# Stick-breaking attention: keys in pairs of 512-blocks, with PSUM banks regrouped to hold the pairs

## The chip, the cores and the metric

One core of one Trainium2 chip runs one program, a whole decoder block. The metric is the device time of one execution in microseconds (us). A kernel is timed several times and the median counts; one more execution is profiled, and its trace shows every instruction of the engines: TensorE (PE in the rows; its weight loads are PEld), VectorE (DVE), ScalarE (ACT), GpSimd (POOL) and SyncE (SP), which issues most of the DMAs.

## What is computed

The block has one input projection, an attention of 8 heads and a pooling branch beside each other, one output projection, and a SwiGLU FFN. The sequence has 2048 tokens, the model 1024 channels, a head 64. The change is in the attention, which for a query t and keys s < t is

```
z = q . k / sqrt(64)
w[t,s] = sigmoid(z[t,s]) * product over s < j < t of sigmoid(-z[t,j])
out[t] = sum over s of w[t,s] * v[s]
```

The reference writes it with logarithms (log_sigmoid and a reversed cumsum); the kernel forms the running product itself, from the last key to the first.

## The kernel before

**Stages.** The program projects the tokens (q, k, v and the pooling input u), then runs the attention with the rest of the projection woven into it, then the output projection, and then the FFN, whose products are arranged as seven instead of eight. The order of the instructions on TensorE, VectorE, ScalarE and GpSimd is the order in which the Python code issues them (tc.manual_schedule); only the waits are set by the framework. Each engine works through its own list in that order, so what stands behind a waiting instruction waits too.

**Units and steps of the attention.** A unit is (h, tb, sc): head h, a block of 512 queries tb, a block of 512 keys sc, with sc from tb down to 0, since the product runs backwards. A unit has four steps i, one for each 128 queries. There are 80 units and so 320 steps. In a diagonal unit (sc == tb) a step has only (i + 1) * 128 keys; in the others it has 512. The loop at L953 issues for step n, in this order:

- weights_step (L792), for step n: two matmuls write the scores z into one PSUM bank (L801, L802; q is held as a high and a low part), and a third adds the causal mask in diagonal units (L804). ScalarE writes sigmoid(z/8) into the SBUF tile sg (L806) and then sigmoid(-z/8) over z in its PSUM bank (L807).
- scan_step (L810), for the step before (it waits until two are in the list, L960): VectorE forms the running product pr with one tensor_tensor_scan over z, from the last key to the first, starting with the first column of the same rows' product in the key block to the right (prevs) or with 1 (L818). GpSimd sets the column right of the product (L815 or L817) and multiplies sg by the shifted product: w (L821).
- values_step (L839), up to LAG turned tiles late: two matmuls add w times v into the bank av (L848, L849), for the high and the low part of w. After the last of a (head, query block), ScalarE copies av out (L853) and SP stores it.
- turn_step (L825), OFF = 7 steps late: TensorE turns up to four 128x128 squares of w into one PSUM bank wt (L833); ScalarE copies the high part wth out (L59), VectorE subtracts it from wt to get the low part wtl (L60).
- filler: pieces of the projection that is left, each of three matmuls (L69 to L71) into the bank mm. How many go into a step follows from the costs at L959 and L967 (2.5 for a step of a diagonal unit, 4.0 for another), so that they end with unit END = 78 of 80. Their results are evacuated by ScalarE, VectorE and GpSimd within the same steps.

**Banks.** All of the program uses one PSUM pool with eight banks of 512 fp32 columns: three for z (ZB), two for wt (WB), one mm, two av. In SBUF the attention has five buffers of sg, six of pr and eleven of w.

**Ends.** The first products of the output projection (mix_pieces) are woven into the last steps of the attention, three pieces a step (PER_STEP).

Of the kernel before, what the change touches and what calls it, by code (L numbers as in the profile page):

```python
# [17 lines left out]
P = 128  # L18
# [26 lines left out]
def block_kernel(ctx, tc, x, c, w_cond, b_cond, g_mix_pre, g_mix_post, w_in, w_pool,  # L45
# [93 lines left out]
    psp = ctx.enter_context(tc.tile_pool(name="ps1", bufs=2, space=PSUM, reuse_waits="tile"))  # L139
# [629 lines left out]

    att = open_pool(ph1, "att", bufs=2)  # L770
# [17 lines left out]
    qts, prevs, avs, wss = {}, {}, {}, {}  # L788
# [3 lines left out]
    def weights_step(u, i):  # L792

        h, tb, sc = u
        diag = sc == tb
        kt, qt = kv[h, sc][0], qts[h, tb]
        L = (i + 1) * P if diag else TB
        nm = f"{h}_{tb}_{sc}_{i}"
        z = z_ps(f"z{nm}")
        keys = kt[:, 0:L]  # L800
        nc.tensor.matmul(z[:, 0:L], qt[:, 0, i * P:(i + 1) * P], keys, start=True, stop=False)  # L801
        nc.tensor.matmul(z[:, 0:L], qt[:, 1, i * P:(i + 1) * P], keys, start=False, stop=not diag)  # L802
        if diag:
            nc.tensor.matmul(z[:, i * P:L], ident_r, neg_r, start=False, stop=True)  # L804
        sg = att.tile([P, TB], F32, tag="sg", bufs=5, name=f"sg{nm}")
        nc.scalar.activation(sg[:, 0:L], z[:, 0:L], AF.Sigmoid, scale=0.125)  # L806
        nc.scalar.activation(z[:, 0:L], z[:, 0:L], AF.Sigmoid, scale=-0.125)  # L807
        scans.append((u, i, z, sg, L, nm))

    def scan_step(u, i, z, sg, L, nm):  # L810

        diag = u[1] == u[2]
        pr = att.tile([P, TB + 1], F32, tag="pr", bufs=6, name=f"pr{nm}")
        if diag:
            nc.gpsimd.memset(pr[:, L:L + 1], 1.0)  # L815
        else:
            nc.gpsimd.tensor_copy(pr[:, L:L + 1], prevs[i][:, 0:1])  # L817
        nc.vector.tensor_tensor_scan(pr[:, 0:L][:, ::-1], z[:, 0:L][:, ::-1], sg[:, 0:L],  # L818
                                     one if diag else prevs[i][:, 0:1], ALU.mult, ALU.bypass)
        w = att.tile([P, TB], F32, tag="w", bufs=OFF + 4, name=f"w{nm}")  # L820
        nc.gpsimd.tensor_tensor(w[:, 0:L], sg[:, 0:L], pr[:, 1:L + 1], ALU.mult)  # L821
        prevs[i] = pr
        wss.setdefault(u, []).append(w)
# [748 lines left out]
```

## Time and profile before

| | |
|---|---|
| median of 3 runs | 2350.9 us (2348.78 to 2353.78) |
| the profiled execution | 2351.43 us, of which the trace spans 2349.6 us |
| granted TensorE clock, mean | 0.991 |
| TensorE busy over the span | 97% |
| VectorE, GpSimd, ScalarE busy | 70%, 55%, 50% |
| attention, first score matmul to last one | 323.5 to 854.3 us |

Busy time is the union of the instructions' spans on an engine. A matmul's span goes from its start to the modelled end of its pipeline, and the next one starts before that, so the busy share of TensorE says little about how much room it has; the distances between starts say more. On the other engines, too, an instruction starts a little before the one ahead of it has ended. A row of a group gives the mean span of one instruction; the advance, from one start to the next, is read from the timeline.

### The profile page before, as it was taken

Reading aid. Unit: us, or ns where it says so; the run is one execution under the profiler, and the core shown is the slowest. Engines: PE = TensorE matmul, PEld = TensorE weight load, DVE = VectorE, ACT = ScalarE, POOL = GpSimd, SP = SyncE. Lnnn points to the kernel's source line nnn. Section 1 sums busy time; section 2 is a strip of 40 time slices with the busy share of each in tenths; the row PEclk is TensorE's granted clock in tenths of the full one; section 3 lists DMA queues with packets and bytes.
Section 4 is the critical chain, followed back from the end, with each engine's and each line's share of the span. In section 5 each row is a group of like instructions: output and inputs, shape, how many; then the busy total and the mean of one; then the engine's idle time right before and its main releaser. Section 6 shows DMA issues by size and latency. Waiting matters only on the chain.

```text
span 2349.6 us, 33532 instructions
## 1 busy us (share of the span) xinstructions
PE 2278.4 (97%) x10717; PEld 1866.6 (79%) x10717; DVE 1638.0 (70%) x2221; ACT 1179.3 (50%) x2411; POOL 1293.3 (55%) x1429
## 2 busy tenths in 40 slices
PE   6999999999999989999999999999999999999997
PEld 3778878888888768887888888788888888888885
DVE  6764549999999975757565565886776565555556
ACT  4323659899998864444222232454533323234444
POOL 4542337787677764544777778430475665641004
PEclk9999999999999999999999999999999999999998
DMA  8785764333443636656554555776763333327554
GB/s 287 244 293 193 273 189 117 90 105 90 126 113 95 190 99 196 220 193 203 163 167 153 162 161 179 264 243 201 257 196 101 119 110 95 114 86 279 193 196 144
DMA packets 307116, 405.18 MB, mean 172 GB/s; under 512 B 19254, under 2 KB 179578, under 8 KB 303868
## 3 DMA queue, kind: packets, MB, share of 16 engines
q1 hardware_dynamic: 302620, 400.68, 52.8%
q10 hardware_dynamic: 4320, 2.36, 0.4%
q8 instruction: 85, 1.39, 0.2%
q14 instruction: 91, 0.75, 0.1%
HBM read 274.51 MB, written 128.45 MB: 171 GB/s over the span
## 4 chain that ended last, share of the span: by engine, by line
PE 79%; DVE 7%; issue 4%; ACT 4%; POOL 3%; DMA 3%; SPq 0%; DVEq 0%; POOLq 0%; ACTq 0%
PE t_u L70 3%; PE t_u L69 3%; PE t_u L71 3%; PE t_g L70 3%; PE t_g L69 3%; PE t_g L71 3%; PE wt L833 3%; PE dn0p L70 3%; PE dn0p L71 3%; PE dn0p L69 3%; PE dn1p L70 3%; PE dn1p L69 3%; PE dn1p L71 3%; DVE pr L818 3%; PE b_g L70 2%
## 5 line engine op out<-in xcount | busy, mean ns | idle before, releaser
L821 POOL TENSOR_TENSOR w<-sg,pr 128x512 f32<-128x512 f32 (+2 forms) x320 | 306.1, 956 | 143.6 <-DVE pr L818 81.3
L1179 POOL TENSOR_TENSOR s<-s,cu 128x512 f32<-128x512 f32 x88 | 132.7, 1515 | 240.7 <-DVE cu L1178 140.1
L818 DVE TENSOR_TENSOR_SCAN pr<-z,pr,sg 128x512 f32<-128x512 f32 x192 | 244.5, 1274 | 0.5 <-POOL pr L817 0.5
L60 DVE TENSOR_TENSOR wtl<-wt,wth 128x512 fp32r<-128x512 f32 (+1 forms) x320 | 190.3, 595 | 35.0 <-ACT wth L59 33.0
L806 ACT ACTIVATE sg<-z 128x512 f32<-128x512 f32 (+2 forms) x320 | 175.0, 547 | 48.0 <-PE z L804 22.2
L59 ACT CAST wth<-wt 128x512 fp32r<-128x512 f32 (+1 forms) x320 | 173.1, 541 | 21.5 <-PE wt L833 19.8
L833 PE MATMUL wt<-ident,w 128*128 128x128 f32 x1088 | 172.0, 273 | 2.5 <-DVE wtl L60 2.2
L807 ACT ACTIVATE z<-z 128x512 f32<-128x512 f32 (+2 forms) x320 | 174.1, 544 | 0.0
L60 DVE TENSOR_TENSOR u_s_l<-u_s,u_s_h 128x512 fp32r<-128x512 f32 x66 | 66.4, 1007 | 151.9 <-ACT u_s_h L59 151.9
L833 PEld LDWEIGHTS wt<-ident,w 128*128 128x128 f32 x1088 | 133.5, 140 | 32.6 <-DVE wtl L60 3.7
L1169 ACT ACTIVATE s<-s 128x512 f32<-128x512 f32 x88 | 55.7, 633 | 192.6 <-DVE s L1168 192.6
L801 PE MATMUL z<-kt,qt 128*128 128x512 f32 (+2 forms) x320 | 128.8, 403 | 16.8 <-DVE pr L818 12.2
L70 PE MATMUL dn0p<-w0p_l,g0p_h 128*128 128x512 f32 x308 | 121.2, 394 | 1.9 <-DVE w0p_l L60 1.9
L848 PE MATMUL av<-wth,vt 128*128 128x512 f32 (+1 forms) x320 | 121.5, 380 | 0.0
L60 DVE TENSOR_TENSOR u_a_l<-u,u_a_h 128x512 fp32r<-128x512 f32 x66 | 77.4, 1175 | 62.3 <-ACT u_a_h L59 62.3
L69 PE MATMUL dn0p<-w0p_h,g0p_h 128*128 128x512 f32 x308 | 120.5, 391 | 0.0
L71 PE MATMUL dn0p<-w0p_h,g0p_l 128*128 128x512 f32 x308 | 120.4, 391 | 0.0
L59 ACT CAST g_s_h<-g_s 128x512 fp32r<-128x512 f32 x66 | 39.5, 620 | 157.6 <-POOL g_s L1111 81.5
L849 PE MATMUL av<-wtl,vt 128*128 128x512 f32 (+1 forms) x320 | 116.9, 365 | 0.0
L802 PE MATMUL z<-kt,qt 128*128 128x512 f32 (+2 forms) x320 | 116.7, 365 | 0.0
L59 ACT CAST u_s_h<-u_s 128x512 fp32r<-128x512 f32 x66 | 38.6, 614 | 152.2 <-POOL u_s L1111 152.2
L70 PE MATMUL dn1p<-w1p_l,g1p_h 128*128 128x512 f32 x292 | 114.4, 392 | 0.0
(655 smaller groups left out, 7266.2 us busy)
## 6 DMA issues: line engine op xcount, KB each, us to landing
g<-in_w_gate_dram SPq DMA_DIRECT2D x42, 512.0 KB, 4.6
u<-in_w_up_dram SPq DMA_DIRECT2D x42, 512.0 KB, 5.0
wc<-in_w_cond_dram SPq DMA_DIRECT2D x32, 512.0 KB, 5.8
qt<-qd SPq DMA_DIRECT2D x64, 256.0 KB, 3.9
wd<-in_w_down_dram SPq DMA_DIRECT2D x44, 256.0 KB, 3.0
tdt<-wd SPq DMA_DIRECT2D x44, 256.0 KB, 2.0
w0p<-tdt SPq DMA_DIRECT2D x44, 256.0 KB, 2.9
w1p<-tdt SPq DMA_DIRECT2D x44, 256.0 KB, 2.8
```

The lines of the kernel that those rows point to most:

```text
L59: nc.scalar.copy(hi, src)
L60: low.tensor_tensor(lo, src, raw(hi), ALU.subtract)
L69: nc.tensor.matmul(ps, lh, rh, start=first and i == 0, stop=False)
L70: nc.tensor.matmul(ps, lh, rl, start=False, stop=False)
L71: nc.tensor.matmul(ps, ll, rh, start=False, stop=last and i == n - 1)
L801: nc.tensor.matmul(z[:, 0:L], qt[:, 0, i * P:(i + 1) * P], keys, start=True, stop=False)
L806: nc.scalar.activation(sg[:, 0:L], z[:, 0:L], AF.Sigmoid, scale=0.125)
L807: nc.scalar.activation(z[:, 0:L], z[:, 0:L], AF.Sigmoid, scale=-0.125)
L818: nc.vector.tensor_tensor_scan(pr[:, 0:L][:, ::-1], z[:, 0:L][:, ::-1], sg[:, 0:L], one if diag else prevs[i][:, 0:1], ALU.mult, ALU.bypass)
L821: nc.gpsimd.tensor_tensor(w[:, 0:L], sg[:, 0:L], pr[:, 1:L + 1], ALU.mult)
L833: nc.tensor.transpose(wt[:, i * P:(i + 1) * P], wss[u][i][:, b * P:(b + 1) * P], ident)
L1179: nc.gpsimd.tensor_tensor(s, s, u, ALU.mult)
```

## The change

A unit now has a list of key blocks: per head ((0, (0,)), (1, (0, 1)), (2, (1, 2)), (2, (0,)), (3, (2, 3)), (3, (0, 1)))), so two neighbouring blocks of 512 keys go together wherever there are two. That makes 48 units and 192 steps. A pair's step writes its scores into two neighbouring PSUM banks (the tile zz), has one sigmoid each way over up to 1024 columns and one scan over them; GpSimd still makes one w for each block. The product that goes on to the next unit is copied into a small tile (carry).

The loop's order changes too. The scan is issued in the step of its scores, not one step later. A step of a pair turns two tiles (each step still turns the share of a unit OFF = 5 steps back), and the two subtractions wtl are issued behind the scan of the step. Values are taken as long as more than LAG tiles wait.

PSUM is split into three pools, one after the other. In the attention there are two buffers of zz (four banks), two wt, one mm and one av, where there were three z, two wt, one mm and two av. SBUF buffers: sg three (each twice as wide), pr three (twice as wide), w six for a unit's first block and eight for its second. The costs by which the filler is spread, its end, and the places where the first output products are loaded, split and multiplied are set anew. The projection ahead of the attention, the output projection's other tiles and the FFN compute the same with the same number of instructions; their banks are taken in turn from eight tags of one bank each.

```diff
-OFF = 7
+OFF = 5
 ZB, WB = 3, 2
+WBUFS = 6, 8
...
+    psst.close()
+    psst = ExitStack()
+    psp = psum_pool(psst, "ps2")
+    z_ps = lambda name: psum("av", 1, name)
+    av_ps = z_ps
+
+    def zz_ps(name):
+        return psp.tile([P, 2, TB], F32, tag="zz", bufs=2, name=name)
...
     def weights_step(u, i):
...
+        zz = zz_ps(f"z{nm}")
+        for p, sc in enumerate(blocks):
+            diag = sc == tb
+            L = (i + 1) * P if diag else TB
+            z, keys = zz[:, p], kv[h, sc][0][:, 0:L]
+            nc.tensor.matmul(z[:, 0:L], qt[:, 0, i * P:(i + 1) * P], keys, start=True, stop=False)
+            nc.tensor.matmul(z[:, 0:L], qt[:, 1, i * P:(i + 1) * P], keys, start=False, stop=not diag)
+            if diag:
+                nc.tensor.matmul(z[:, i * P:L], ident_r, neg_r, start=False, stop=True)
+        W = (len(blocks) - 1) * TB + L
+        z = zz.rearrange("p b k -> p (b k)")[:, 0:W]
+        sg = att.tile([P, 2 * TB], F32, tag="sg", bufs=3, name=f"sg{nm}")
+        nc.scalar.activation(sg[:, 0:W], z, AF.Sigmoid, scale=0.125)
+        nc.scalar.activation(z, z, AF.Sigmoid, scale=-0.125)
...
     def scan_step(u, i, z, sg, W, nm):
...
+        pr = att.tile([P, 2 * TB + 1], F32, tag="pr", bufs=3, name=f"pr{nm}")
+        carry = carries.pop(i, None)
+        if carry is None:
+            nc.gpsimd.memset(pr[:, W:W + 1], 1.0)
         else:
+            nc.gpsimd.tensor_copy(pr[:, W:W + 1], carry)
+        nc.vector.tensor_tensor_scan(pr[:, 0:W][:, ::-1], z[:, ::-1], sg[:, 0:W],
+                                     one if carry is None else carry, ALU.mult, ALU.bypass)
+        if blocks[0]:
+            carries[i] = att.tile([P, 1], F32, tag=f"carry{i}", bufs=2, name=f"carry{nm}")
+            nc.gpsimd.tensor_copy(carries[i], pr[:, 0:1])
+        for p in range(len(blocks)):
+            cols = slice(p * TB, min((p + 1) * TB, W))
+            w = att.tile([P, TB], F32, tag=f"w{p}", bufs=WBUFS[p], name=f"w{nm}_{p}")
+            nc.gpsimd.tensor_tensor(w[:, 0:cols.stop - cols.start], sg[:, cols],
+                                    pr[:, cols.start + 1:cols.stop + 1], ALU.mult)
...
+    units = [(h, tb, blocks) for h in range(HEADS) for tb, blocks in
+             ((0, (0,)), (1, (0, 1)), (2, (1, 2)), (2, (0,)), (3, (2, 3)), (3, (0, 1)))]
+    cost = {1: 1.7, 2: 3.5}
+    area = [cost[len(blocks)] - (0.6 if blocks[-1] == tb else 0) for _, tb, blocks in units]
...
-    END = 78
+    END = 0.965
...
-    PER_STEP = 3
+    PER_STEP = 2
...
             weights_step(u, i)
-            spent += 2.5 if u[1] == u[2] else 4.0
-        if len(scans) > 1 or n >= len(steps) and scans:
-            scan_step(*scans.pop(0))
-        if len(waiting) > LAG:
+            spent += area[n // 4]
+        while len(waiting) > LAG:
             values_step(*waiting.pop(0))
         if n >= OFF:
-            u, b = steps[n - OFF]
-            waiting.append((u, b, *turn_step(u, b)))
-        goal = START + (N_PIECES - START) * spent / (4 * sum(area[:END]))
+            u, i = steps[n - OFF]
+            for m in range(i * len(u[2]), (i + 1) * len(u[2])):
+                parts, low = turn_step(u, m // 4, m % 4)
+                waiting.append((u, m // 4, m % 4, *parts))
+                turned_lows.append(low)
+        if scans:
+            scan_step(*scans.pop(0))
+        while turned_lows:
+            turned_lows.pop(0)()
+        goal = START + (N_PIECES - START) * spent / (4 * END * sum(area))
```

More of the change, by code (lines that the diff above doesn't have):

```diff
@@ L786, in block_loads @@
         return qt
-    qts, prevs, avs, wss = {}, {}, {}, {}
+    qts, carries, avs, wss = {}, {}, {}, {}
     scans = []
     def weights_step(u, i):
[L794 to L808, printed above, removed]
@@ L857, in unit_loads @@
     def unit_loads(u):
-        h, tb, sc = u
-        if sc == tb:
+        h, tb, blocks = u
+        if blocks[-1] == tb:
             qts[h, tb] = block_loads(h, tb)
@@ L949, in mix_pieces @@
                 count -= 1
-    waiting = []
+    waiting, turned_lows = [], []
     spent = 0.0
```

70 lines of the change are left out of this document (38 added, 32 removed).

## The prediction

> **What bounds the kernel now.** I read the page first, then the table of stretches, then the waits and the groups by shape of the attention, and last the timeline of a few microseconds in it.
>
> ```profile
> PE   6999999999999989999999999999999999999997
> ...
> DVE  6764549999999975757565565886776565555556
> ```
>
> The 40 slices are 58.7 us each. TensorE is at nine tenths nearly everywhere; VectorE is there with it only in slices 7 to 14, the attention. The profiled execution took 2351.43 us, 0.5 above the median of the runs (2350.9), so I add to the former and leave the 0.5 alone. The stage in stretches:
>
> ```profile
> 370.00:822.00 452.00, 442.92 (x2535) 368.84 (x2534) 428.17 (x548) 406.66 (x898) 331.82 (x606) 1.00 0.41 118
> 822.00:840.00 18.00, 15.35 (x86) 11.78 (x85) 17.08 (x23) 15.58 (x35) 16.41 (x27) 1.00 0.66 205
> 840.00:860.00 20.00, 15.77 (x82) 11.57 (x81) 20.00 (x24) 17.01 (x35) 14.38 (x24) 1.00 0.32 96
> 323.30:860.00 536.70, 517.32 (x2943) 427.92 (x2942) 506.53 (x647) 479.52 (x1056) 392.79 (x716) 1.00 0.41 119
> ```
>
> The columns are length, then busy time of PE, PEld, DVE, ACT, POOL, then granted clock, DMA share, GB/s. The last row is the attention: 536.7 us for eight heads, **67.1 us a head**, with PE busy 517.3, DVE 506.5, ACT 479.5. Two engines are full at once, so taking work from VectorE alone gives little; TensorE leaves at most 536.7 - 517.3 = 19.4 us.
>
> ```profile
> DVE wtl L60 <- ACT wth L59: 27.3, 60, 2.3
> ...
> PEld wt L833 <- DVE wtl L60: 3.7, 4, 2.7
> ```
>
> These are two waits of the attention (total us, times, longest). VectorE's largest is for ScalarE's high part, 27.3 us in all. TensorE's turns wait for a bank of the turned weights to be read (wtl) four times in 320 steps; this row matters below.
>
> **The change part by part.**
>
> ```profile
> L821 POOL TENSOR_TENSOR w<-sg,pr 128x512 f32<-128x512 f32 x224 | 244.8, 1093 | 102.3 <-DVE pr L818 59.3 <-ACT sg L806 20.9 <-ACT wth L59 3.4
> L818 DVE TENSOR_TENSOR_SCAN pr<-z,pr,sg 128x512 f32<-128x512 f32 x192 | 244.5, 1274 | 0.5 <-POOL pr L817 0.5
> ...
> L60 DVE TENSOR_TENSOR wtl<-wt,wth 128x512 fp32r<-128x512 f32 x220 | 148.6, 675 | 23.4 <-ACT wth L59 22.0
> L806 ACT ACTIVATE sg<-z 128x512 f32<-128x512 f32 x224 | 137.0, 611 | 30.4 <-PE z L802 18.6 <-PE z L804 6.6 <-POOL pr L815 1.4
> ...
> L818 DVE TENSOR_TENSOR_SCAN pr<-z,ones,sg 128x128 f32<-128x128 f32 x32 | 15.1, 473 | 0.0
> ...
> L806 ACT ACTIVATE sg<-z 128x128 f32<-128x128 f32 x32 | 9.6, 299 | 4.0 <-PE z L804 3.1 <-POOL pr L817 0.6
> ```
>
> ```profile
> 404.90 1.27 DVE L818 TENSOR_TENSOR_SCAN pr<-z,pr,sg 128x512 f32<-128x512 f32 x1
> ...
> 406.09 0.66 DVE L60 TENSOR_TENSOR wtl<-wt,wth 128x512 fp32r<-128x512 f32 x1
> ...
> 406.67 1.27 DVE L818 TENSOR_TENSOR_SCAN pr<-z,pr,sg 128x512 f32<-128x512 f32 x1
> ```
>
> *Fewer scans.* A scan costs (1274 - 473) / 384 = 2.09 ns a column. In the timeline one of 512 columns advances VectorE by 406.09 - 404.90 = 1.19 us, of which 512 x 2.09 = 1.07 are columns and 0.12 is fixed. 320 scans become 192 with the same columns: 128 x 0.12 = **15 us less on VectorE**. A scan over 1024 columns and two banks is in no row. Its bounds are the 1.27 of one bank and twice that, 2.55; I take the line, 1.27 + 1.07 = 2.34, which lies nearest to the two.
>
> *Fewer sigmoids.* (611 - 299) / 384 = 0.81 ns a column, so 1024 columns take 0.61 + 0.42 = 1.03 us (bounds 0.61 and 1.22). Against 2 x 0.61 that takes at most 0.19 off each of 256 merges, less where they overlap. ScalarE isn't last, so I credit nothing.
>
> *GpSimd* makes the same 320 products; 128 settings of a single column go and 64 carries of a single column come, beside its idle time: nothing.
>
> *TensorE* issues exactly as many instructions as before. *One value bank:* ScalarE's copy of av now has to end before the next block's first value matmul; that comes a whole step later, behind turns, filler and scores, while the copy has only the step's two sigmoids ahead of it, so I cost it at nothing (its cover is that step of over 2 us; without it up to 1 us, 31 times). DMAs and their places by step are the same; head and tail I take as they are, up to 5 us either way (PE's idle time in the two tail stretches is 2.65 + 4.23 us).
>
> *The new order* is what decides. In each step VectorE now does the scan, then the subtractions of the tiles turned in that step, and a pair's step turns two tiles through the two wt banks. So TensorE can turn the next step's second tile only when VectorE has ended this step's second subtraction, which stands behind this step's scan. Behind those turns on TensorE stand the filler and then the scores of the step after next, whose sigmoids and scan follow. That closes a **loop of two steps**. Its prices:
>
> ```profile
> 754.19 0.39 PE L849 MATMUL av<-wtl,vt 128*128 128x512 f32 x1
> 754.20 0.59 PEld L833 LDWEIGHTS wt<-ident,w 128*128 128x128 f32 x4
> ...
> 754.42 0.60 PE L833 MATMUL wt<-ident,w 128*128 128x128 f32 x4
> ...
> 754.78 0.48 PE L69 MATMUL u<-hth,wu_h 128*128 128x512 f32 x1
> ...
> 755.56 0.40 PE L801 MATMUL z<-kt,qt 128*128 128x512 f32 x1
> ...
> 757.75 0.39 PE L802 MATMUL z<-kt,qt 128*128 128x512 f32 x1
> ...
> 758.24 0.60 ACT L806 ACTIVATE sg<-z 128x512 f32<-128x512 f32 x1 [0.45 <-PE z L802]
> ...
> 758.73 0.59 ACT L807 ACTIVATE z<-z 128x512 f32<-128x512 f32 x1
> ```
>
> A matmul advances TensorE by 0.23 (754.19 to 754.42), four turns by 0.36, a filler piece of three matmuls by 0.78 (754.78 to 755.56). A weight load comes 0.22 ahead of its turn. The wait from the end of a score matmul (757.75 + 0.39) to the sigmoid is 0.10, and I take 0.2 for the loop's three changes of engine together. Filler: the code has 24 products of 8 pieces, 192, and START puts 31 of them ahead of the attention; 161 are left in it, 161 x 0.78 = 126 us, spread by the new costs, which add up to 60 a head: 126 / 480 = 0.26 us for a unit of cost.
>
> Per head 24 steps, in three classes of eight:
>
> - *Pair of key blocks, two tiles turned* (880 columns on average). Scan 0.12 + 880 x 0.00209 = 1.96. Subtractions: full tiles 0.58 + 0.67, with the narrow tiles of the diagonal 1.10. Hops 0.2 and weight load 0.22. Four turns or fewer, 0.30. Filler 3.1 x 0.26 = 0.82. Four score matmuls and the mask, 0.97 to the end of the last. Sigmoids: the first advances by 0.49 for 512 columns, 0.79 for 880, and the second takes 0.91: 1.70. Together 7.27, **3.64 a step**. TensorE's own work is 3.2 (scores 0.87, values 0.84, turns 0.68, filler 0.82), VectorE's 3.0.
> - *One key block, two tiles turned* (416 columns). The same sum: 0.99 + 1.15 + 0.42 + 0.33 + 0.37 + 0.57 + 0.93 = 4.76, 2.38 a step; TensorE's own work is 2.37. Two limits as near as that add up a little: 2.5.
> - *Pair of key blocks, one tile turned.* The second wt bank takes the wait out of the loop. TensorE has 2.4, VectorE 2.5; over the 95% that VectorE reached in the middle (428.17 of 452.00), 2.6.
>
> 8 x (3.64 + 2.5 + 2.6) = 69.9 us a head.
>
> *The ring of w.* The buffers of a unit's first block are six steps deep. Unit (2, (0,)) is read by turns until three steps after its first one, so GpSimd has to hold the products of the third and fourth step of the next pair until the fourth turn is done. Behind it come three products of 1.09, 3.3 us, before the next pair can be turned, where filler, scores and values take 0.8 + 0.9 + 0.5 = 2.2: TensorE is 1.1 late, once a head.
>
> Sum: 71.0 against 67.1 us a head, 3.9 x 8 = **31 us more**, 2351.4 + 31 = **2383 us** (rounded up). The old order had no such loop: the scan stood a step behind its scores, three z banks lay ahead of it, and one tile a step was turned through the two wt banks. Scan, subtraction, turns, filler, scores, sigmoids (1.19 + 0.67 + 0.42 + 0.36 + 0.50 + 0.62 + 1.10 = 4.9) were spread over four steps of 1.7, and the row of four waits says the same.
>
> **The rivals.**
>
> - *The loop isn't tight (faster).* One mechanism decides: whether the two-bank scan and sigmoids take what the line says. At its lower bound the scan is 1.27 and not 2.34 for a full pair, and the first class falls to 3.1, under TensorE's 3.2. From a loop shorter by some 0.45 a step, TensorE is the bound with the room that VectorE's 15 us give it. It can win no more than its 19.4 us idle; three quarters of that make 2337. For it: the columns of the scan are the largest term and I extend a line. Against it: four widths lie on that line.
> - *No change (2351).* The loop binds in full pairs alone, and the 31 us are cancelled by what VectorE's and ScalarE's new room saves elsewhere: that would have to be all of the 27.3 us of waits for wth. The classes would have to lie at 2.3 to 2.4 for the last two, and TensorE's own work doesn't allow much of that.
> - *More waits than counted.* Loop and ring meet: the late pair turns hold VectorE's subtractions and so the next loop, and filler pieces fall in lumps of 0.78. If every step takes the larger of its two-step loops, another 3 to 4 us a head: 2351 + 60 = 2411.
> - *The clock.* TensorE would wait some 0.4 us in every pair step. In the tail (822 to 860) it was idle for 15 to 21% and its clock stayed at 1.00, which speaks against a loss. Were the clock at the 0.94 of the stretch from 117 to 176 us,
>
> ```profile
> 117.48:176.22 58.74, 56.48 (x251) 46.85 (x250) 40.87 (x46) 16.80 (x35) 26.07 (x29) 0.94 0.89 293
> ```
>
>   TensorE's third of the loops would grow by 6%, 2% of 570 us: 11 more, 2394, inside the range. The Trainium skill ("TensorE: Matmul & The Clock Gate", section "A second HAM failure mode: psum-queue depth-cycling") says that frequent micro-idles between groups of matmuls that cycle through PSUM banks make the gate swing between half and full clock. By that rule the same pattern would cost more than my 11; the tail rows don't bear it out.
>
> **How the numbers follow.** Chances: loop as computed 0.66 (2362 to 2400), more waits 0.10 (to 2415), clock 0.03, no change 0.06, faster 0.15. A measurement of this kernel can tell about 0.2%, 5 us. That gives faster 0.15, same 0.06, slower 0.79. The range reaches from 2346, which takes in no change, to 2415, and leaves out most of the faster case and the worst of the waits.
>
> **What would show it.** In the profile after: scans of 1024 columns at about 2.34 us and 128 fewer instructions on VectorE; VectorE's busy time in the attention lower by some 15 us, but idle ahead of scans, with ScalarE's second sigmoid as the releaser; a new large wait of TensorE's turns for wtl (hundreds of times, not 4); GpSimd waiting for TensorE's turns eight times, once a head; pair steps of full blocks of about 4 us; the clock at 1.00. I am wrong if the turns wait for wtl no more than now, if the scan of 1024 columns takes under 2 us, or if TensorE is busy over 97% of the attention again.

## The result and the profile after

The changed kernel takes **2415.07 us** (median of 4 runs, 2412.44 to 2416.8) against 2351.49 (2348.78 to 2353.78) for the kernel before: ratio **1.027**, interval 1.0252 to 1.0288, so 64 us slower. The forecast was 31 us slower. The profiled execution took 2412.44 us, its span is 2410.6.

The attention in the table of stretches: the six middle heads, then from the first score matmul to some 5 us behind the last one, as in the row of the kernel before. Columns as before: length; busy PE, PEld, DVE, ACT, POOL; clock; DMA share; GB/s.

```profile
392.98:847.55 454.57, 414.49 (x2272) 331.45 (x2271) 377.80 (x397) 351.06 (x614) 286.97 (x494) 1.00 0.36 102
323.70:917.00 593.30, 534.80 (x2921) 425.97 (x2919) 492.61 (x513) 459.06 (x796) 379.19 (x652) 0.99 0.37 105
```

The attention lasts 593.3 us instead of 536.7, 56.6 more. The six middle heads, 454.57 us, are 75.8 each; the same six take 403.7 us, 67.3 each, in the kernel before (385.85 to 789.58 us). VectorE is busy 492.6 us instead of 506.5, so it did get its 14 us back, and TensorE, ScalarE and VectorE are now all idle for 58 us or more. No engine is the bound by its busy time. The clock is at 0.99 to 1.00.

The shapes in the groups of the attention (us busy, mean ns):

```profile
L836 DVE TENSOR_TENSOR_SCAN pr<-z,carry,sg 128x1024 f32<-128x1024 f32 x32 | 75.1, 2346 | 16.4 <-ACT z L824 6.6 <-POOL w L844 4.6 <-POOL u L377 4.1
...
L823 ACT ACTIVATE sg<-z 128x1024 f32<-128x1024 f32 x56 | 57.8, 1033 | 26.3 <-PE z L817 15.9 <-PE z L819 8.0 <-POOL pr L835 1.0
```

A scan over 1024 columns in two banks takes 2.35 us and a sigmoid 1.03; the line gave 2.34 and 1.03. The sizes of the operations are therefore not where the missing 33 us are. The waits of the attention (total us, times, longest):

```profile
PEld wt L856 <- DVE wtl L860: 65.4, 119, 1.9
...
ACT sg L823 <- PE z L819: 54.4, 75, 2.1
...
PE wt L856 <- DVE wtl L860: 35.3, 46, 1.5
DVE pr L836 <- ACT z L824: 34.5, 31, 3.1
...
PEld z L816 <- DVE pr L836: 24.1, 29, 1.6
...
POOL w L844 <- PE wt L856: 14.0, 8, 1.9
...
PE z L816 <- DVE pr L836: 12.9, 21, 1.3
```

The turns wait for the subtraction in 119 weight loads and 46 matmuls (a load and its matmul can wait for the same thing, so the two don't add up to one number); before it was 4 loads and 1 matmul. GpSimd waits for a turn eight times, once a head, 1.7 to 1.9 us each: the ring. And there is a wait that the forecast did not price: the **score matmuls wait for the scan** (24.1 and 12.9 us).

The turn loop in the timeline of a full pair, one engine after the other: start, length, and in brackets the idle time before.

```profile
610.01 0.65 PE L856 MATMUL wt<-ident,w 128*128 128x128 f32 x4 [1.11 <-DVE wtl L860]
...
613.05 1.18 PE L856 MATMUL wt<-ident,w 128*128 128x128 f32 x8
613.99 0.48 PE L70 MATMUL k<-hth,wk_h 128*128 128x512 f32 x1
...
615.46 0.40 PE L816 MATMUL z<-kt,qt 128*128 128x512 f32 x1
```

```profile
610.00 2.35 DVE L836 TENSOR_TENSOR_SCAN pr<-z,carry,sg 128x1024 f32<-128x1024 f32 x1
612.26 1.26 DVE L860 TENSOR_TENSOR wtl<-wt,wth 128x512 fp32r<-128x512 f32 x2
614.41 2.35 DVE L836 TENSOR_TENSOR_SCAN pr<-z,carry,sg 128x1024 f32<-128x1024 f32 x1 [0.89 <-POOL w L844]
616.68 1.26 DVE L860 TENSOR_TENSOR wtl<-wt,wth 128x512 fp32r<-128x512 f32 x2
618.69 2.35 DVE L836 TENSOR_TENSOR_SCAN pr<-z,carry,sg 128x1024 f32<-128x1024 f32 x1 [0.75 <-POOL w L844]
```

```profile
616.65 1.03 ACT L823 ACTIVATE sg<-z 128x1024 f32<-128x1024 f32 x1 [0.85 <-PE z L817]
617.57 1.03 ACT L824 ACTIVATE z<-z 128x1024 f32<-128x1024 f32 x1
```

Scan from 610.00, both subtractions to 613.52, and in the block of eight turns from 613.05 the last four, which need the second subtraction, from 613.58 on; then two filler pieces, the scores from 615.46, the sigmoids to 618.60, the scan of two steps later at 618.69: 8.69 us for two steps. The row names GpSimd's w as the releaser of that scan, but GpSimd's last w had ended at 614.57, and the scan starts 0.09 us after the second sigmoid's end (617.57 + 1.03 = 618.60). Its idle time ends there, as the prediction said.

This holds beyond the one pair. In the six middle heads VectorE is idle for more than 0.15 us ahead of 92 scans, and every one of them starts 0.10 us or less behind the end of a second sigmoid. Of the 97 such pauses of ScalarE ahead of a first sigmoid, 96 end as close behind a score matmul, so neither GpSimd nor the SBUF buffers hold these two. Of TensorE's 64 waits ahead of a turn that are longer than 0.15 us, 57 end 0.05 to 0.06 us behind the end of a subtraction.

The second loop, in pair steps that turn one tile:

```profile
600.81 0.50 PE L816 MATMUL z<-kt,qt 128*128 128x512 f32 x1
...
603.48 0.50 PE L816 MATMUL z<-kt,qt 128*128 128x512 f32 x1
```

```profile
598.94 1.82 DVE L836 TENSOR_TENSOR_SCAN pr<-z,ones,sg 128x768 f32<-128x768 f32 x1 [1.07 <-ACT z L824]
...
601.34 2.08 DVE L836 TENSOR_TENSOR_SCAN pr<-z,ones,sg 128x896 f32<-128x896 f32 x1
```

One scan ends at 598.94 + 1.82 = 600.76 and the scores that use its tile again start at 600.81; the next ends at 603.42 and its scores start at 603.48. With two score tiles and the scan in its own step, the scores of step n+2 can't start before scan n has ended. All 15 waits of TensorE ahead of scores that are longer than 0.15 us in the six middle heads end 0.05 to 0.06 us behind the end of a scan. From there to the end of scan n+2 stand scores, two sigmoids and a scan: 0.06 + 1.2 + 0.10 + 1.94 + 0.09 + 2.35 = 5.7 us for a full pair, 2.9 a step.

From the starts of TensorE's instructions in the six middle heads (48 steps of each class) follows where it works and where it stands. A step goes from one score matmul to that of the next step; what exceeds the advance of an instruction (0.23 us for 512 columns, 0.11 for one turn of 128) by more than 0.15 us counts as waiting, and belongs to the instruction behind it. Shorter delays stay in the own work; counted from 0.06 us on, they would move 0.1 to 0.2 us a step from the own work to the waits. All in us a step:

| class | forecast | measured | own work | waits: turned weights | score tile | value bank |
|---|---|---|---|---|---|---|
| pair, two tiles turned | 3.64 (and the ring, 0.14) | 3.87 | 3.34 | 0.48 | 0 | 0.04 |
| one key block, two tiles turned | 2.5 | 2.76 | 2.39 | 0.37 | 0 | 0.01 |
| pair, one tile turned | 2.6 | 2.83 | 2.59 | 0.01 | 0.19 | 0.04 |

TensorE's own work in a head is 8 x (3.34 + 2.39 + 2.59) = 66.6 us. The same reckoning of the trace of before gives 65.3 us of own work and 2.0 of waits for scores in a middle head of 67.3. So the work is 1.3 us more, and the waits have grown from 2.0 to 9.1: 8 x (0.48 + 0.37 + 0.01) = 6.9 us a head for turned weights, 8 x 0.19 = 1.5 for score tiles, 0.7 for the value bank.

Within the second class the wait isn't spread evenly. The first step behind a full pair waits 1.17 and 1.09 us (there are two such steps in a head), the other six 0.12 on average: the turns of that step stand behind the scan and the subtractions of the pair before it.

### The profile page after: what moved, and what is told of

It reads as the page before. It is cut to its first block, busy times and chain, and to the rows that moved or that the text cites. A ratio compares the mean times of both kernels' runs of the same rounds, so it can differ in the third digit from the quotient of the medians.

```text
span 2410.6 us, 32183 instructions
## 1 busy us (share of the span) xinstructions
PE 2299.4 (95%) x10717; PEld 1867.8 (77%) x10717; DVE 1625.2 (67%) x2093; ACT 1160.4 (48%) x2155; POOL 1281.5 (53%) x1365
## 4 chain that ended last, share of the span: by engine, by line
PE 61%; POOL 3%; DVE 2%; issue 2%; ACT 1%; DMA 1%; DVEq 0%; POOLq 0%; ACTq 0%; SPq 0%
PE t_u L72 3%; PE t_u L71 3%; PE t_u L70 3%; PE t_g L71 3%; PE t_g L70 3%; PE t_g L72 3%; PE dn0p L71 3%; PE dn0p L72 3%; PE dn0p L70 3%; PE dn1p L71 3%; PE dn1p L70 3%; PE dn1p L72 3%; PE b_g L71 2%; PE b_u L71 2%; PE b_u L70 2%; PE b_g L72 2%
## 5 line engine op out<-in xcount | busy, mean ns | idle before, releaser
L836 DVE TENSOR_TENSOR_SCAN pr<-z,ones,sg 128x896 f32<-128x896 f32 (+7 forms) x128 | 215.2, 1681 | 71.0 <-POOL w L844 19.5
L856 PE MATMUL wt<-ident,w 128*128 128x128 f32 x1088 | 168.7, 281 | 41.2 <-DVE wtl L860 35.3
L823 ACT ACTIVATE sg<-z 128x640 f32<-128x640 f32 (+3 forms) x192 | 150.2, 783 | 94.8 <-PE z L819 54.4
L856 PEld LDWEIGHTS wt<-ident,w 128*128 128x128 f32 x1088 | 123.6, 141 | 87.7 <-DVE wtl L860 65.4
L860 DVE TENSOR_TENSOR wtl<-wt,wth 128x512 fp32r<-128x512 f32 (+1 forms) x320 | 179.2, 594 | 9.1 <-ACT wth L859 8.7
L859 ACT CAST wth<-wt 128x512 fp32r<-128x512 f32 (+1 forms) x320 | 158.7, 531 | 45.8 <-PE wt L856 44.5
L61 DVE TENSOR_TENSOR u_s_l<-u_s,u_s_h 128x512 fp32r<-128x512 f32 x66 | 65.4, 991 | 151.9 <-ACT u_s_h L60 151.9
L824 ACT ACTIVATE z<-z 128x640 f32<-128x640 f32 (+3 forms) x192 | 149.2, 777 | 0.0
L836 DVE TENSOR_TENSOR_SCAN pr<-z,carry,sg 128x512 f32<-128x512 f32 (+1 forms) x64 | 116.0, 1813 | 27.5 <-ACT z L824 15.8
L816 PE MATMUL z<-kt,qt 128*128 128x512 f32 (+2 forms) x320 | 121.9, 381 | 13.3 <-DVE pr L836 12.9
L70 PE MATMUL dn1p<-w1p_h,g1p_h 128*128 128x512 f32 x292 | 114.2, 391 | 0.0
```

The lines of the kernel that those rows point to most:

```text
L61: low.tensor_tensor(lo, src, raw(hi), ALU.subtract)
L70: nc.tensor.matmul(ps, lh, rh, start=first and i == 0, stop=False)
L823: nc.scalar.activation(sg[:, 0:W], z, AF.Sigmoid, scale=0.125)
L824: nc.scalar.activation(z, z, AF.Sigmoid, scale=-0.125)
L836: nc.vector.tensor_tensor_scan(pr[:, 0:W][:, ::-1], z[:, ::-1], sg[:, 0:W], one if carry is None else carry, ALU.mult, ALU.bypass)
L856: nc.tensor.transpose(wt[:, i * P:(i + 1) * P], wss[u, p][i][:, b * P:(b + 1) * P], ident)
```

## The experiments

The expectations number their theories. Theory 1 is the turn loop of the prediction; theory 2 is that the score tiles, held from scores to scan, set the step; theory 3 is that the buffers of GpSimd's products do; theory 4 is that the filler comes in lumps too large. A to D are explained in their texts. Where only a ratio's interval tells two kernels apart, it is given.

### In the changed kernel

**Filler ahead of the turns.** The filler's matmuls and the evacuations that belong to it are issued before the turns.

```diff
             values_step(*waiting.pop(0))
+        goal = START + (N_PIECES - START) * spent / (4 * END * sum(area))
+        while fill is not None and taken < goal:
...
         if n >= OFF:
```

> The changed kernel with the filler pieces issued ahead of the turns of the same step instead of behind them; nothing else moves. Theory 1 (the two-step loop scan, subtractions, turns, filler, scores, sigmoids, scan): the filler leaves the loop, 0.82 / 2 = 0.41 us for each of 64 pair steps that turn two tiles and 0.37 / 2 = 0.19 for each of 64 single steps, 38 us less: about 2377. Theory 2 (coarse grain alone: two score tiles of two banks, and scan, scores, sigmoids, scan in a row, wherever filler and turns stand): no change, 2410 to 2420. Theory 3 (TensorE and VectorE wait for GpSimd through the rings of w and pr): no change either.

Measured 2406.17 us, ratio 1.0229 (1.021 to 1.0248): 9 less than the changed kernel. The pairs that turn two tiles fell from 3.87 to 3.54 us a step, as theory 1 wants, but the other two classes rose by 0.10 and 0.07: the evacuations now stand ahead of the scans on VectorE and wait there for ScalarE's half (10.6 us for k and 9.0 for q, where the changed kernel had 6.3 for k and no such row for q).

**Only the filler's matmuls ahead of the turns**, the evacuations behind.

```diff
...
-                run_small()
+                if attending:
+                    behind.append(run_small)
+                else:
+                    run_small()
...
+        while behind:
+            behind.pop(0)()
```

> As e6_filler_first, but only the filler's matmuls move ahead of the turns; its evacuations and weight splits on ScalarE, VectorE and GpSimd stay behind the subtractions, where the changed kernel has them. In e6_filler_first the class of pair steps with two tiles turned fell from 3.80 to 3.48 us, as the turn loop says, while the other two classes rose by 0.05 and 0.14 and VectorE waited for evacuations ahead of scans. Theory 1 (the turn loop): without that side effect the gain of the first class stays and nothing rises: (0.32 + 0.1) x 64 = 27 us under the changed kernel, about 2388. If filler in the loop were not the cause, no better than e6_filler_first, 2406.

2399.82 us, ratio 1.0201 (1.0184 to 1.0218): 15 less, the best version with pairs, and still 48 slower than the kernel before. The turns' waits for the subtraction shrink from 65.4 and 35.3 us to 44.1 and 19.6:

```profile
PEld wt L862 <- DVE wtl L866: 44.1, 91, 1.9
...
PE wt L862 <- DVE wtl L866: 19.6, 27, 1.5
```

In pairs that turn two tiles TensorE waits 0.19 us a step for turned weights instead of 0.48; with one key block it stays at 0.37, of which the first step behind a pair makes the most (1.30 and 1.13 us). So the turn loop does cost, and loosening it gave 15 us, about half of the 27 that theory 1 expected.

**The subtractions ahead of the scan.** This takes the scan out of the turn loop.

```diff
-        if scans:
-            scan_step(*scans.pop(0))
         while turned_lows:
             turned_lows.pop(0)()
+        if scans:
+            scan_step(*scans.pop(0))
```

> The changed kernel with the subtractions of a step issued ahead of its scan instead of behind it. Theory 1: the turn loop is cut, because a turn no longer stands behind a scan; but the scan then stands behind ScalarE's copies of this step's turns, which come after its sigmoids: scan, scores, sigmoids, two copies, subtraction, scan is 7.3 us in two full steps, little less than the 8.3 of the loop that is cut, and single steps lose some. 2395 to 2425. Theory 2 (the score loop alone: scan, scores, sigmoids, scan): this lengthens it by two copies and a subtraction, 1.7 us in two steps, so 2440 or more.

2436.05 us, ratio 1.0357: 21 slower than the changed kernel, above the range of theory 1 and 4 us below that of theory 2. The waits show what took the loop's place:

```profile
DVE wtl L860 <- ACT wth L859: 125.6, 136, 3.3
...
PE z L816 <- DVE pr L836: 52.1, 52, 2.2
```

The turns hardly wait for turned weights any more (0.09, 0.06 and 0 us a step). Instead VectorE stands still for ScalarE's high part, the scan comes later, and the score matmuls wait for it, 52.1 us where it was 12.9. By class, in the order of the table, TensorE's wait for score tiles went from 0, 0 and 0.19 us a step to 0.16, 0.49 and 0.57.

**The scan one step later**, as in the order before.

```diff
-        if scans:
+        if len(scans) > 1 or n >= len(steps) and scans:
             scan_step(*scans.pop(0))
```

> The changed kernel with the scan issued one step later, as the kernel before had it. Theory 1: the loop then closes over three steps, 7.3 / 3 = 2.4 us, under what TensorE needs for a pair step (3.2); most of the 64 us go: 2350 to 2375. Theory 2: a later scan holds the two score tiles a step longer, so no better: 2415 or more.

2441.17 us, ratio 1.0374: 26 slower, on theory 2's side.

```profile
DVE wtl L860 <- ACT wth L859: 122.8, 135, 2.8
...
PE z L816 <- DVE pr L836: 59.6, 51, 3.0
...
PEld wt L856 <- DVE wtl L860: 6.1, 21, 1.1
```

The turn loop is gone (6.1 us) and the time is worse. The scan ends later, each score tile is held longer, and there are only two: 0.22, 0.53 and 0.59 us a step of waits for score tiles. That the turn loop alone holds the step (theory 1) falls here: there are two loops, and either edit opens the one by tightening the other.

**The merged operations undone.** Each block of a pair has its own sigmoids and scan again, within the same step, and the right block's scores are issued first.

```diff
...
-        nc.scalar.activation(sg[:, 0:W], z, AF.Sigmoid, scale=0.125)
-        nc.scalar.activation(z, z, AF.Sigmoid, scale=-0.125)
+        for p in reversed(range(len(blocks))):
+            cols = slice(p * TB, min((p + 1) * TB, W))
+            nc.scalar.activation(sg[:, cols], z[:, cols], AF.Sigmoid, scale=0.125)
+            nc.scalar.activation(z[:, cols], z[:, cols], AF.Sigmoid, scale=-0.125)
...
+        for p in reversed(range(len(blocks))):
+            cols = slice(p * TB, min((p + 1) * TB, W))
+            nc.vector.tensor_tensor_scan(pr[:, cols][:, ::-1], z[:, cols][:, ::-1], sg[:, cols],
+                                         start, ALU.mult, ALU.bypass)
```

> The changed kernel with the merge undone inside the step: each key block has its own sigmoids and its own scan again, the right block first; banks, order and steps stay. VectorE gets its 128 x 0.12 = 15 us back. Theories 1 and 2 both say that the row scores, sigmoids, scan gets shorter, since the right block's scan runs beside the left block's sigmoids: by 5.4 - 4.3 = 1.1 us in two full steps, 0.5 x 64 = 35 us: about 2380. If the engines' work bounded the steps, it would be 10 to 15 us slower.

2451.07 us, ratio 1.0419: 36 slower, where both theories had some 35 faster. The first scan was meant to start while the second block's sigmoids run; it did not, in any of the 128 pair steps. In a full pair of its trace the second block's sigmoids end at 640.93 and the first scan starts at 641.03. So the sigmoids take 2.21 us instead of 1.94 and the scans 2.60 instead of 2.35, all of it inside both loops. The merge by itself is worth some 36 us in this order; what surrounds it costs more.

**Eight buffers of w for a unit's first block**, and five instead of six of kt and vt to make room.

```diff
-WBUFS = 6, 8
+WBUFS = 8, 8
...
```

> The changed kernel with eight instead of six buffers of w for a unit's first block (and, for room, five instead of six of the key and value blocks). Theory 1 gives the ring 1.1 us a head: 9 us less, 2406. Theory 3 gives it and what it delays behind it half of the loss: 2385 or less. With the ring off every path: no change.

2408.37 us, ratio 1.0238 (1.0218 to 1.0258): 7 less. GpSimd's eight waits for a turn are gone. The ring was priced at 9 us. Theory 3, which had 2385 or less here, falls.

**Filler by single matmuls** instead of pieces of three.

```diff
...
+                    nc.tensor.matmul(ps, w[1][:, k, :], hi, start=k == 0, stop=False)
+                    yield 1 / 3
...
```

> The changed kernel with the filler of the attention spread by single matmuls instead of pieces of three; order, counts and costs stay. Theory 4 (no room to run ahead: with two score tiles and the scan in its own step, each step takes the larger of TensorE's time with its lump of filler, 0 to 1.6 us, and the loops, where the kernel before let them average): even filler saves a part of that, 10 to 30 us: 2385 to 2405. Theory 1 alone (the mean length of the turn loop): the same filler in the same loops, 2408 to 2420.

2409.97 us, ratio 1.0247 (1.0232 to 1.0263): 5 less, within theory 1's range. Theory 4 falls; the lumps cost 5 us, not half of the miss.

### The new order without pairs

**One key block to a unit.** Everything else of the change stays: its order, two score tiles, one value bank, five steps from scores to turns.

```diff
-WBUFS = 6, 8
+WBUFS = 12, 2
...
-             ((0, (0,)), (1, (0, 1)), (2, (1, 2)), (2, (0,)), (3, (2, 3)), (3, (0, 1)))]
+             [(tb, (sc,)) for tb in range(NTB) for sc in range(tb, -1, -1)]]
```

> The changed kernel with its new order, its two score tiles and its one value bank, but units of one key block each, as before (320 steps; twelve buffers of w in one ring). Nothing is merged, each step turns one tile. Theories 1 and 2 both say that the loops need the pair: with one tile a step the turn loop closes over three steps, and the score loop is (0.1 + 0.6 + 0.1 + 1.1 + 0.1 + 1.2) / 2 = 1.6 us a step against 1.7 of work: 2345 to 2375. If the order of the scan and the subtractions, or the one value bank, cost by themselves: 2395 or more.

2388.83 us, ratio 1.0156 (1.0141 to 1.0172), 37 slower than the kernel before, between the two ranges that were expected. So the new order loses time without any pair. It isn't the same loss as that of the changed kernel, where turned weights make most of the waits, and the 37 can't be taken off the 64. The waits here:

```profile
PEld z L816 <- DVE pr L836: 51.2, 108, 1.5
...
PE z L816 <- DVE pr L836: 20.0, 39, 1.2
PEld av L872 <- ACT o L877: 14.0, 28, 1.1
```

TensorE waits for score tiles, and for the copy of the one value bank. The same kernel with **filler by single matmuls**, the edit shown above:

> As e16_new_order_single (2389: the new order with one key block a step) with the filler spread by single matmuls. There a full step with a piece of filler took 2.0 to 2.2 us (TensorE) and one without 1.78 (the score loop and VectorE), while TensorE's mean is 1.8. Theory 4: even filler takes most of that away: 2350 to 2370. If the loops' mean length sets the time: 2380 to 2390.

2381.8 us, ratio 1.0123 (1.0103 to 1.0144), 7 less, in the range without theory 4: the lumps are not it here either. Which of the rest makes the 37 us was then tried one at a time. **Four score tiles** of one bank each (there each of the two held a second bank that it didn't use), with six sg and six pr:

```diff
-        return psp.tile([P, 2, TB], F32, tag="zz", bufs=2, name=name)
+        return psp.tile([P, 1, TB], F32, tag="zz", bufs=4, name=name)
...
-        sg = att.tile([P, 2 * TB], F32, tag="sg", bufs=3, name=f"sg{nm}")
+        sg = att.tile([P, TB], F32, tag="sg", bufs=6, name=f"sg{nm}")
...
-        pr = att.tile([P, 2 * TB + 1], F32, tag="pr", bufs=3, name=f"pr{nm}")
+        pr = att.tile([P, TB + 1], F32, tag="pr", bufs=6, name=f"pr{nm}")
...
```

> The new order with one block of 512 keys to a unit (2388.8 us with two score tiles) now gets four score tiles of one bank each in the same eight banks (there each tile held a second bank that it didn't use), and the buffers sg and pr are six of one block each instead of three of two. The scan stays in the step of its scores, one value bank stays. Theory A (score tiles: with two of them and the scan in its own step, the scores of step n+2 can't start before scan n ends, which couples TensorE, ScalarE and VectorE): the 71 us of waits of the score matmuls for pr go, and the time falls to 2350 to 2362. Theory B (the one value bank, 14.0 + 2.7 us of waits for the copy o): stays above 2380. Theory C (filler and its costs, carries): stays above 2380.

2382.39 us, ratio 1.0126 (1.0103 to 1.0148). By the time, theory A falls and B or C is left. Yet the waits for score tiles went, as A said, and others stand in their place, for the copy of the value bank, for the subtraction and for GpSimd:

```profile
PEld av L872 <- ACT o L877: 21.2, 29, 1.8
...
PEld wt L856 <- DVE wtl L860: 19.6, 34, 1.6
...
PEld wt L856 <- POOL w L844: 13.9, 29, 1.2
PEld wt L856 <- POOL pr L833: 12.6, 21, 1.8
```

**The control**, six sg and pr with two score tiles (bufs=2 in the same diff):

> Control for the run with four score tiles: the same kernel (new order, one key block to a unit, sg and pr six deep, one bank to a score tile), but still two score tiles. Theory A: 2385 to 2391, as with three sg and pr, since the score matmuls wait for the scan and not for SBUF. If the depth of sg and pr is what costs, it falls to 2350 to 2365 here already.

2390.65 us, ratio 1.0156 (1.0131 to 1.018): the depth in SBUF is nothing. **Two value banks** with two score tiles:

```diff
...
-    z_ps = lambda name: psum("av", 1, name)
+    z_ps = lambda name: psum("av", 2, name)
...
-        return psp.tile([P, 2, TB], F32, tag="zz", bufs=2, name=name)
+        return psp.tile([P, 1, TB], F32, tag="zz", bufs=2, name=name)
...
```

> The new order with one key block to a unit and two score tiles (2388.8 us), but with two value banks, as the old order has them. Theory A: the first value matmul no longer waits for the copy o (14.0 + 2.7 us in the waits), but most of that comes back as waits for score tiles: 2380 to 2388. Theory B (the value bank is the cause): below 2372.

2391.99 us, ratio 1.0156 (1.013 to 1.0182): 4 above the range of theory A. (The 2.7 us in the text on record is a row of the changed kernel; in this order the wait of the value matmuls for the copy is 4.9 us, beside the 14.0 of their weight loads.) The waits for the copy go and come back as waits for score tiles (59.4 and 25.0 us, where they were 51.2 and 20.0). Theory B falls as the cause of the 37 us; a cost that the score tiles hide isn't excluded by this run. **Four score tiles with the scan a step later** (the diff of the scan one step later, on top of the four tiles):

> Four score tiles, one key block to a unit, and the scan one step later, as in the old order; one value bank, the subtractions behind the scan, the new costs of the filler and the carries stay. Theory A: within 6 us of the time of the kernel before, 2345 to 2357, and then nothing of the new order but the pairing of score tiles and scans with too few banks costs time. Theory C (filler costs, carries, place of the subtractions): 2365 or more.

2461.93 us, ratio 1.0462. This miss gave the missing part:

```profile
PEld wt L856 <- POOL w L844: 67.3, 60, 2.4
PE wt L856 <- POOL w L844: 53.2, 54, 2.2
PEld wt L856 <- POOL pr L833: 38.3, 26, 2.2
PE wt L856 <- POOL pr L833: 32.3, 26, 2.0
```

The turns wait for GpSimd. The first turn of a unit takes a column of squares from all four of its w, so five steps late it needs the one scored two steps ago; with the scan a step later that product has only just been started. (The rows that name pr are the same wait: GpSimd sets a column of pr right behind w. Under both names TensorE's idle time, but for a single turn, ends 0.05 us behind the end of a w.) In the old order it was seven steps. So **seven steps instead of five**, with four and with two score tiles:

```diff
-OFF = 5
+OFF = 7
```

> One key block to a unit, four score tiles, scan in its own step, one value bank as in the run with four score tiles (2382.4 us), but the turns come seven steps late instead of five. A unit's first turn needs the products w of all four of its steps, so at five steps late it needs the one of two steps ago, of which GpSimd is just then at work; in the run with four tiles the turns waited 40.5 us for GpSimd's w or for what stands behind it, in the run with the scan a step later 191 us. Theory D (two couplings, each enough to hold the step: two score tiles with the scan in its own step, and the short distance from product to turn): 2353 to 2365. Theory B or C (one value bank, carries, costs of the filler): 2375 or more.

> The same distance of seven steps with two score tiles (2388.8 us at five steps). Theory D: the score tiles still hold it, 2380 to 2390. If the distance alone were the cause: 2353 to 2365.

With four tiles 2361.95 us, ratio 1.0039 (1.0024 to 1.0054); with two 2381.78, ratio 1.0118 (1.0102 to 1.0135). Both lie where theory D put them, and B and C fall with the former: one value bank, the carries and the filler's costs together have at most the 9 us that are left. The waits of the latter:

```profile
PEld z L816 <- DVE pr L836: 55.4, 115, 1.7
...
PE z L816 <- DVE pr L836: 21.4, 39, 1.4
```

and in the former that pair of rows is down to 0.8 us:

```profile
PEld z L816 <- DVE pr L836: 0.8, 2, 0.5
```

Slower than the kernel before by, in us (from the medians, with the kernel before of the same chip, 2351.4 to 2353.4):

| | five steps to the turns | seven steps |
|---|---|---|
| two score tiles | 37 | 28 |
| four score tiles | 29 | 9 |

Either coupling alone costs some 20 us above the 9, and both together 28: a step that waits for one of them has the other one free. In the version with 9 us the turns wait for the subtractions (31.1 us in weight loads, 18.5 in matmuls) and the values for the copy of the one bank (15.3 and 5.9); whether these make the 9 wasn't tried.

### In the kernel before

**The scan in its own step**, with its three score banks:

```diff
-        if len(scans) > 1 or n >= len(steps) and scans:
+        if scans:
             scan_step(*scans.pop(0))
```

> The kernel before with the scan issued in the step of its scores, as the change does; three score banks, one tile a step and the lumps of filler stay. Theory 4: the third bank still lets TensorE run ahead, but VectorE has a step less between scores and scan: 2351 to 2370. If the scan's place were the cause by itself: 2380 or more.

2356.95 us, ratio 1.0027 (1.0017 to 1.0038): 6 slower, with 35.6 us of waits of the turns' loads for the subtractions. The turn loop is there, and with one tile a step, three score banks and seven steps it costs almost nothing.

**Two score banks** and **one value bank** were to be had in the kernel before by asking for an extra tile, which is never used, between the used ones:

```diff
         z = z_ps(f"z{nm}")
+        if i % 2:
+            z_ps(f"idle{nm}")
```

```diff
             avs[h, tb] = av_ps(f"av{h}_{tb}")
+            av_ps(f"idle{h}_{tb}")
```

> The kernel before with two score banks in the attention (the third is left idle); its order, lag and filler stay. The score loop over two steps is (0.06 + 0.6 + 0.1 + 1.1 + 0.1 + 1.2) / 2 = 1.6 us a step, under the work of 1.7. Theory 4: the loss of run-ahead costs all the same, 2365 to 2395. Theories 1 and 2 by mean lengths: 2351 to 2358.

> The kernel before with one value bank in the attention (each second buffer of av is left idle); nothing else moves. My working gives the one bank nothing. In the profile after TensorE waited 4.9 + 2.7 us for ScalarE's copy of av. So 2351 to 2360; if the value bank is a cause of its own, 2370 or more.

2351.85 us (0.9997, 0.9987 to 1.0007) and 2350.78 us (0.9998, 0.9988 to 1.0007). Both are inconclusive. The score matmuls of the first wait for what they waited for before (12.8 us for the scan against 12.2), so the unused tile seems to have taken no bank. They show only how well the time of one and the same work repeats, within 0.1%.

## Why the prediction was wrong

The direction, the turn loop and the sizes of the operations were right. The sum was 33 us short, because two of the three classes were priced too low and a second loop, through the score tiles, was not seen.

- *Fewer scans.* 15 us less on VectorE forecast, 13.9 measured (506.5 to 492.6 us of busy time in the attention). 1024 columns at 2.35 us against 2.34. That this alone gains nothing was right, yet the merge was priced as VectorE's relief only: within the step its operations lie in series in both loops, and undoing it, right block first, costs 36 us.
- *GpSimd, the value bank.* Both priced at nothing. A second value bank gave nothing in the order without pairs; in the changed kernel TensorE waits 0.7 us a head for the copy, and a second bank was not tried there.
- *The ring.* Eight waits, priced at 9 us; 7 measured.
- *Pairs that turn two tiles.* 3.87 us, where the loop gave 3.64 and the ring 0.14: the turn loop is in the trace with the parts that the prediction named. 0.09 x 64 steps = 6 us short.
- **One key block, two tiles turned: the term that was mis-sized most**, "Two limits as near as that add up a little: 2.5". It is 2.76; TensorE's own 2.39 is near the 2.37 forecast, and the waits are 0.37 a step, not 0.13. I priced each class as if it ran by itself. But this one lasts four steps at a time, and the first one's turns wait for the scan and the subtractions of the full pair before it, and it has only one block's scores and little filler to put in that time. 0.26 x 64 = 17 us.
- **Pairs that turn one tile: the step that failed**, "The second wt bank takes the wait out of the loop. TensorE has 2.4, VectorE 2.5; over the 95% that VectorE reached in the middle (428.17 of 452.00), 2.6". The turns indeed hardly wait there (0.01). But TensorE's own work is 2.59, not 2.4. The parts that the prediction gives (scores 0.87, half of the values and turns, filler 0.82) make 2.45 already. Values lag two tiles, so the first step behind two turned tiles still has four value matmuls: two of eight steps, 0.11 on average. And scores, sigmoids and scan of two steps share two tiles, a loop of 2.9 us a step for full pairs, which I did not write down: 0.19 of wait for score tiles. 0.23 x 64 = 15 us.
- Together 6 + 17 + 15 = 38 us for eight heads like the middle ones, against the 33 that were missing. The middle six lose 454.6 - 403.7 = 51 of the attention's 56.6 us, so the first and the last lose less. The other 4 us of the profiled difference (2410.6 against 2349.6) lie behind it.
- *The old order "had no such loop".* With the scan moved into its own step the kernel before does show a turn loop, at 6 us; the reasons given, three score banks and a scan a step behind, agree with that. The prediction did not ask what two tiles and a scan in its own step do to the scores.
- *Rivals.* 2411 for "more waits than counted" came nearest, 4 us off, in part by chance: of its reasons, the lumps of filler (5 us) and the ring (7 us) are small, and it doesn't name the score tiles. "The loop isn't tight" is excluded by the scan's 2.35 us. The clock stayed at 0.99 to 1.00 in the attention, with the 119 and 29 waits of weight loads above, so it isn't the cause. The rule cited from the Trainium skill ("TensorE: Matmul & The Clock Gate", section "A second HAM failure mode: psum-queue depth-cycling") is that frequent micro-idles make the clock swing; this trace shows no such loss. Versions with more waits had a slightly lower clock, 0.98 over the stretch of the six middle heads with the merge undone and 0.985 over the whole run with four tiles and the scan a step later, against 0.991 before; whether the waits do that wasn't tried.

What stays open: that the score loop stands ready behind the turn loop was shown for pairs by opening the latter, and by the trace, not by giving pairs a third tile. No version with pairs opens both loops at once, so what the two cost together there is read from TensorE's waits, not measured as a time. Six banks for scores, two for turned weights, one for the filler and one for values would be ten of eight, so that wasn't tried. The coupling by five steps matters in the order without pairs; in the changed kernel the turns wait for w in few places:

```profile
PEld wt L856 <- POOL w L844: 5.8, 6, 2.3
```

No version beat the kernel before.

## What to carry to other kernels

When buffers and order change together, write down for each pool what has to end before its next tile can be written, and close every such chain through the engines into a loop; a step takes at least as long as the longest of these loops, however idle the engines are, and not only the loop that was seen first counts. Where steps of different sizes alternate every few steps, price the change from one to the next too: a small step pays for the large one that stands ahead of it. Two loops of nearly the same length hide each other: removing either one took 8 or 9 us off the 37 here, and only removing both showed what they cost (9 left). Merging operations in series shortens such a loop, but when it takes the banks that kept the steps apart, more can be lost than the saved instructions were worth, as here.

## What the runs showed of the hardware

- One scan and one sigmoid over two neighbouring PSUM banks run at the rate of one bank, with no step at the boundary: scans of 384, 512, 640, 768, 896 and 1024 columns take 1.02, 1.28, 1.55, 1.82, 2.08 and 2.35 us, sigmoids of 512 and 1024 columns 0.61 and 1.03.
- The changes of engine inside the loops are short: 0.05 to 0.06 us from the end of a scan, a subtraction or a product on GpSimd to the matmul that waits for it, 0.09 to 0.10 from a score matmul's modelled end to the sigmoid and from the sigmoid to the scan. The loops are long because of the work in them.
- In the run with the merge undone, a scan of one block did not start before the sigmoids of the other block, in the other bank of the same tile, had ended: 0.09 us at the least lay between them in all 128 pair steps. Whether the wait comes from sharing one tile or from something else wasn't tried.
